# Two-layer decoder trunk, one core: which pairs of output tiles are multiplied by Strassen's scheme at the turns between stages

## Chip, cores, metric

One Trainium2 chip, one NeuronCore. The metric is device microseconds per execution; three executions of the kernel before took 2191.34, 2192.50 and 2198.03 us (median 2192.5).

## What is computed

Each of two layers does, for 512 prompt columns and 8 sample columns together (T = 520, D = 2048, fp32):

```
h = rmsnorm(x) * norm_g
z = h @ w_in
y_conv = B * conv3(C * xc) * silu(g_conv)
y_ret  = groupnorm(retention(q, k, v)) * silu(g_ret)
x = x + concat(y_conv, y_ret) @ w_out
x = x + sigmoid(x @ w_pg) * (p @ w_ple)
```

The four big products (w_in for the heads, w_in for the convolution, w_out, w_pg) hold nearly all the arithmetic.

## The kernel before, in words

Everything is held transposed: a tile is 128 features by 520 columns, and a matrix product has 16 input tiles (K tiles, KT = 16) and is made two output tiles at a time, a **pair**. Precision: every fp32 operand is split into a high and a low part (`split`, line 547; ACT writes the high part, DVE the rest), every weight tile too (`split_w`, line 226), and each product is three matmuls (`mm3`, lines 245 to 247) of 128x128 by 128x260, once for the LEFT and once for the RIGHT half of the columns.

A pair is made in one of two ways (`pair`, line 405). **Plain** (`plain`, line 281): K outermost, in four chunks of four K tiles; four PSUM banks are open from the first to the last chunk, and the banks are emptied only by whoever uses the result. It takes 16 x 4 x 3 = 192 matmuls. **Strassen** (`strassen`, line 303) with s of the 16 K tiles: seven products over s/2 K pairs, the rest of the K tiles plain, 192 - 1.5 s matmuls. It needs sums of weight tiles (DVE, line 328), sums of operand tiles (`operand_sums`, line 420: four DVE instructions of 128x260 per K pair; then `split_sums`, line 429: two ACT and two DVE instructions of 128x520), and inside the pair it moves banks about: `copy` and `plus` (traced at line 316) empty or duplicate banks on ACT and DVE, six ACT copies and two DVE additions where s is under 16, and the next product into that bank waits for them.

How many K tiles of each pair go by Strassen stands in tables: HEADS, CONVS, OUT_ROWS, GATES, one number per pair and layer, in the order in which the pairs run. The program runs heads, convolution, output projection (out), gate, and then the same for layer 1.

The operands of a stage are an `Operands` object with a list of things still to build (`todo`, lines 461 to 464): for each of 8 K pairs the split tiles, the sums, or both at once. `FIRST` says for how many tiles (4, so 2 K pairs) the sums are made together with the split tiles; the sums of the others come later from tiles that are loaded again, and have to be there before the first pair that uses them (`need`, line 494). `fill` builds ahead while enough of the 75 slots are free (it wants 7 above a reserve for a pair with sums). In the last pair of a stage the next stage's operands are built while its own are given back: `free` (line 517) gives back at steps 1, 3, 6, 7 and 8 of a Strassen pair, and all at the end of a plain one. `release` (line 504) gives back sums that no later pair uses. The final order on each engine is set by a scheduler from the program order, data and priorities; every engine then works through its own list in order.

The code of the pair and of what is built when:

```
first = max(rows[0], min(FIRST, max(rows))) // 2
self.todo = [(True, True)] * first + [(True, False)] * (KT // 2 - first)
...
self.todo += [(i, False, True) for i in range(first, max(rows) // 2)]
```

Of the kernel before, what the change touches and what calls it, by code (L numbers as in the profile page):

```python
# [47 lines left out]
SPREAD = (0, 6)  # L48


HEADS = [[0, 0, 0, 4, 8, 12] + [14] * 10, [4, 8, 12] + [14] * 13]
CONVS = [[14] * 2 + [16] * 13 + [14]] * 2
OUT_ROWS = [[0, 8, 16, 16, 16, 16, 16, 10]] * 2

MIXED, MIX = 64, [*range(8, 14), *range(8), 14, 15]
OUTS = [[MIXED + s for s in r] for r in OUT_ROWS]
GATES = [[4, 8, 12, 16, 16, 16, 16, 10], [4, 8, 12] + [14] * 4 + [0]]
WPRIO = 20
LATE = 0
RAW = 32  # L60
WARM = 8
FIRST = 4
SPLIT = 60


# [12 lines left out]
class Slots:  # L78
# [8 lines left out]
    def get(self, dtype=F32):  # L87
        i = self.free.pop(0)
        self.count += 1
        t = self.pool.tile([P, T], dtype, tag=f"s{i}", name=f"slot{i}_{self.count}")  # L90
        self.used[id(t)] = (t, i)
        return t
# [4 lines left out]
    def put(self, *slots):  # L97
        for t in slots:
            self.free.append(self.used.pop(id(t))[1])
# [90 lines left out]
def trunk_kernel(  # L190
# [17 lines left out]
    get, getr, put = slots.get, slots.getr, slots.put  # L208
# [22 lines left out]
    def chunks(a, b, most=CH):  # L231

        n = (b - a + most - 1) // most
        e = [a + (b - a) * i // n for i in range(n + 1)] if n else [a]
        return list(zip(e, e[1:]))

    def parts(src, a, b, slot=False):
        raw = load(src[:, P * a : P * b])
        w = split_w(raw, slot)
        raw_ring.put(raw)  # L240
        return w
# [9 lines left out]
    def product(out, w, c, xs, start, stop, more=False):  # L251

        for i, (xh, xl) in enumerate(xs):
            m = slice(P * (c + i), P * (c + i) + P)
            mm3(out, w[0][:, m], w[1][:, m], xh, xl, start and i == 0, stop and i == len(xs) - 1, more)

    def at(ops, ks, n):
        return [ops[k].view(n) for k in ks]

    def acc(n):  # L260
        return [banks.get() for _ in range(n)]

    def aside():

        if later:
            later.pop(0)()
# [11 lines left out]
            split_ring.put(*w)  # L278
        return Val(banks.put, ps=ps)

    def plain(x, src0, src1):

        ps = acc(4)
        for a, b in chunks(0, KT):
            x.supply(min(b + CH, KT))
            for i, src in enumerate((src0, src1)):
                w = parts(src, a, b)
                for j in range(a, b):
                    for h, n in enumerate((LEFT, RIGHT)):
                        product(ps[2 * i + h], w, j - a, at(x.ops, [j], n), j == 0, j == KT - 1)  # L290
                split_ring.put(*w)
            if b == KT // 2:
                while middle:
                    middle.pop(0)()
                aside()
        aside()
        return Val(banks.put, ps=ps[:2]), Val(banks.put, ps=ps[2:])
# [107 lines left out]
    def pair(x, src, m, n, nxt=None):  # L405


        s = x.rows[n]
        last = n == len(x.rows) - 1 and nxt is not None
        if s:  # L410
            z = strassen(x, src[m], src[m + 1], s, (lambda i: x.free(i, nxt)) if last else None)
        else:
            z = plain(x, src[m], src[m + 1])
            if last:
                x.free(8, nxt)
        x.release(n + 1)
        if nxt is not None and not last and not x.todo:
            nxt.fill(1, PRE)
        return z
# [14 lines left out]
    class Operands:  # L434


        def __init__(self, rows, load, reserve=0, whole=False, gain=None):
# [4 lines left out]
            self.ready = 0  # L442
            first = max(rows[0], min(FIRST, max(rows))) // 2
            self.todo = [(True, True)] * first + [(True, False)] * (KT // 2 - first)
# [72 lines left out]
        def free(self, i, nxt):  # L517

            s = self.rows[-1]
            if not self.whole:  # L520
                for n in range(s // 2):
                    x, y, t = self.ops[2 * n], self.ops[2 * n + 1], self.sums[n][4]
                    if i == 1 and x.halves:
                        put(*x.slots)
                        x.slots = []
                    if i == 3:
                        put(*t[:2])
                        del t[:2]
                    if i == 6:
                        put(*y.slots)  # L530
                        y.slots = []
                    if i == 7:
                        put(*t)
                        t.clear()
            if i == 8:
                self.drop()
            nxt.fill()

        def drop(self):
# [25 lines left out]
    def norm_g(l, k):  # L565
        return vec[:, 16 * l + k : 16 * l + k + 1]
# [97 lines left out]
    def from_dram(src):  # L664
        def load(k):
            t = get()
            SIDE.dma_start(t, src[k])
            return t

        return load  # L670

    xs = []
    X = Operands(HEADS[0][2:] + CONVS[0], from_dram(xT), gain=lambda k: norm_g(0, k))
    X.todo = [t for t in ((i, False, True) for i in range(max(X.rows) // 2))]
    X.ready = KT // 2
    rms = Rms()
    for a, b in ((0, 1), (1, 4), (4, 8), (8, 12), (12, 16)):
        raws = []
        if b == 1:
# [3 lines left out]
            x = get()  # L683
# [5 lines left out]
        else:  # L689
            for i in range(max(b - a, 3)):  # L690
                if i < 3:
                    raws.append(load(wi[0, i, :, P * a : P * b]))
                if i < b - a:
                    x = get()
# [24 lines left out]
    for l in range(DEPTH):  # L719
# [83 lines left out]
        def head(m):  # L803
            middle.append(lambda: X.fill(MORE_HEAD, 0))
            if m // 2 % 2:
                middle.append(sample)
            zs = pair(X, wi[l], m, m // 2 - skipped)
            X.fill(MORE_HEAD, 0)
            X.need(m // 2 - skipped + 1)
            sample()  # L810
            return zs
# [262 lines left out]

        O = Operands(OUT_ROWS[l], mixer, RESERVE_OUT)

        for j in range(CJ):
# [13 lines left out]
            t = get()  # L1091
# [37 lines left out]

        Gt = Operands(GATES[l][: (KT - tail) // 2], gate_in, RESERVE_GATE, whole=bool(tail))  # L1130
        for m in range(0, KT, 2):
# [20 lines left out]
        for k in range(2):  # L1152
            t = get()
# [20 lines left out]
        if not tail:  # L1174
            X = Operands(HEADS[l + 1] + CONVS[l + 1], next_in, RESERVE_NEXT, gain=lambda k, l=l: norm_g(l + 1, k))
        for m in range(0, KT - tail, 2):
# [10 lines left out]
            for i, z in enumerate(zs):  # L1187
                x = xs[i]
                t = get() if z.slot is None else z.slot
# [17 lines left out]
        if tail:  # L1207
# [53 lines left out]
            def update(x, pe, ps):  # L1261
                sg = get()
                t = sg[:, : x.shape[-1]]
                S.activation(t, ps, AF.Sigmoid)
                banks.put(ps)
                V.tensor_tensor(t, t, pe, MUL)
                V.tensor_tensor(x, x, t, ADD)
                return sg, t
# [5 lines left out]
            for i in range(tail):  # L1274
                ps = banks.get(TF)
                for c, w in enumerate(ws):
                    for k in range(2):
                        o, m = ops[2 * c + k], slice(PC * k + P * i, PC * k + P * i + P)
                        mm3(ps, w[0][:, m], w[1][:, m], o.x[:, n0], o.y[:, n0], c + k == 0, c + k == 8)
                x = x2[m0 + i][:, n0]  # L1280
                with tc.high_priority():
                    sg, t = update(x, pes[i][:, n0], ps)
# [15 lines left out]
            for j, n in enumerate(blocks):  # L1298
# [17 lines left out]
                x = xts[:, c]  # L1316
                with tc.high_priority():
                    sg, t = update(x, pts[:, c], ps)
# [147 lines left out]
```

## Time and profile before

| | |
|---|---|
| median of three executions | 2192.5 us |
| the profiled execution | 2188.46 us |
| its span on the core | 2186.6 us |
| mean granted TensorE clock | 0.997 of 2.4 GHz |
| matmuls recorded | 17870 |
| DMA, mean over the span | 179 GB/s |

The profiled execution lies 4.0 us under the median. Stages of the span: heads of layer 0 to about 460 us, convolution to 700, out from about 700 to 875, gate to 1090; heads of layer 1 to 1500, convolution to 1750, out to 1955, gate to the end. A *turn* below is the last pair of one stage and the first of the next.

### The profile page before, as it was taken

To read this page: it belongs to the slowest core of one execution; us is meant where nothing else is said; L and a number is where in the kernel's file an instruction comes from. 1 tells how busy PE (TensorE), PEld (TensorE's weight loads), DVE (VectorE), ACT (ScalarE), POOL (GpSimd) and SP (SyncE) were. 2 spreads that over 40 slices of the span, in tenths; PEclk is the share of its full clock that TensorE was granted. 3 is DMA by queue.
4 is the path that set the end of the run, shared out by engine and by line. 5 is a ranking of instruction groups with operands and counts; after the bars stand their busy time and mean duration, and the time that the engine had idled before them with its cause. 6 is when DMAs were issued, how large, how long until landed. Compare 5 with 4: busy or idle time off the path is not lost.

```text
span 2186.6 us, 48458 instructions
## 1 busy us (share of the span) xinstructions
PE 2155.9 (99%) x17870; PEld 2148.5 (98%) x17870; DVE 1902.8 (87%) x3910; ACT 1282.4 (59%) x2735; POOL 441.8 (20%) x764
## 2 busy tenths in 40 slices
PE   9999999999999999999999999999999999999998
PEld 8999999999999999999999999999999999999998
DVE  8789999899999988888897998989998999888874
ACT  8555666555555655655775565555645565455655
POOL 3213232211001311210211222222110032021011
PEclk9999999999999999999999999999999999999999
DMA  7656575545443853754645566664465456456455
GB/s 258 193 169 200 176 219 185 179 155 175 153 133 125 275 171 122 244 167 160 227 128 179 166 209 195 199 207 158 148 183 150 125 182 220 153 190 209 134 156 195
DMA packets 187918, 392.09 MB, mean 179 GB/s; under 512 B 26592, under 2 KB 66528, under 8 KB 187680
## 3 DMA queue, kind: packets, MB, share of 16 engines
q1 hardware_dynamic: 133040, 214.30, 31.4%
q0 software_dynamic: 54496, 174.62, 24.0%
q8 instruction: 140, 2.29, 0.4%
q14 instruction: 98, 0.80, 0.1%
q10 hardware_dynamic: 144, 0.08, 0.0%
HBM read 323.74 MB, written 65.15 MB: 178 GB/s over the span
## 4 chain that ended last, share of the span: by engine, by line
PE 86%; DMA 5%; issue 3%; ACT 3%; DVE 3%; POOL 1%; SPq 0%; DVEq 0%; ACTq 0%; POOLq 0%
PE ps_g L245 27%; PE ps_g L247 27%; PE ps_g L246 27%; DMA raw<-wg 1%; ACT split L227 1%; DVE split L228 1%; DMA o_rets<-slot 1%; DMA slot<-x2s 1%; DMA slot<-xT 1%; ACT slot L553 1%; DMA raw<-wi 0%; DVE raw L328 0%; POOL slot L1060 0%; DMA raw<-wo 0%; ACT slot L476 0%
## 5 line engine op out<-in xcount | busy, mean ns | idle before, releaser
L245 PE MATMUL ps_g<-slot,split 128*128 128x260 f32 x5500 | 1543.0, 284 | 18.5 <-ACT ps_g L316 8.1
L246 PE MATMUL ps_g<-slot,split 128*128 128x260 f32 x5500 | 1546.1, 283 | 0.3 <-DVE slot L557 0.3
L247 PE MATMUL ps_g<-slot,split 128*128 128x260 f32 x5496 | 1531.4, 283 | 0.6 <-DVE split L228 0.6
L227 ACT ACTIVATE split<-raw 128x512 fp32r<-128x512 f32 (+2 forms) x1388 | 783.2, 584 | 618.5 <-DVE raw L328 199.8
L245 PEld LDWEIGHTS ps_g<-slot,split 128*128 128x128 f32 x5500 | 1031.5, 189 | 22.9 <-ACT ps_g L316 9.2
L246 PEld LDWEIGHTS ps_g<-slot,split 128*128 128x128 f32 x5500 | 1036.7, 189 | 0.5 <-DVE slot L557 0.5
L247 PEld LDWEIGHTS ps_g<-slot,split 128*128 128x128 f32 x5496 | 1028.0, 189 | 0.9 <-DVE split L228 0.8
L228 DVE TENSOR_TENSOR split<-raw,split 128x512 fp32r<-128x512 f32 (+2 forms) x1387 | 848.5, 633 | 182.6 <-ACT split L227 112.8
L328 DVE TENSOR_TENSOR raw<-raw 128x512 f32<-128x512 f32 (+2 forms) x680 | 427.1, 640 | 20.3 <-DMA raw<-wi 13.5
L316 ACT ACTIVATE slot<-ps_g 128x260 f32<-128x260 f32 x360 | 135.6, 379 | 125.2 <-PE ps_g L247 110.5
L554 DVE TENSOR_TENSOR slot<-slot,slot 128x520 fp32r<-128x520 f32 (+1 forms) x206 | 120.3, 615 | 3.9 <-ACT slot L553 3.1
L553 ACT ACTIVATE slot<-slot 128x520 fp32r<-128x520 f32 (+1 forms) x206 | 106.6, 565 | 12.5 <-DVE slot L425 4.4
L783 POOL DMA_DIRECT2D o_rets<-slot x64 | 35.4, 553 | 338.5 <-DVE slot L782 121.3
L316 DVE TENSOR_TENSOR slot<-ps_g,slot 128x260 f32<-128x260 f32 x180 | 75.9, 422 | 5.9 <-PE ps_g L247 3.8
L1060 POOL DMA_DIRECT2D slot<-x1s x82 | 44.0, 538 | 144.1 <-DVE slot L554 51.7
L871 POOL DMA_DIRECT2D slot<-hs x64 | 46.2, 723 | 112.5 <-PE ps_st L247 31.0
L316 ACT ACTIVATE ps_g<-ps_g 128x260 f32<-128x260 f32 x140 | 52.1, 372 | 19.1 <-PE ps_g L247 18.6
L741 DVE TENSOR_TENSOR slot<-slot,slot 128x520 f32<-128x520 f32 x80 | 55.5, 693 | 8.8 <-DMA o_rets<-slot 7.8
L782 DVE SCALAR_TENSOR_TENSOR slot<-slot,vs,slot 128x256 f32<-128x256 f32 x128 | 56.0, 478 | 7.0 <-ACT slot L778 6.3
L816 POOL DMA_DIRECT2D hs<-slot x64 | 35.6, 557 | 129.9 <-DVE slot L757 59.7
L772 POOL DMA_DIRECT2D slot<-sret x64 | 35.3, 552 | 131.4 <-ACT split L227 33.4
L773 POOL DMA_DIRECT2D slot<-kq x64 | 34.8, 544 | 118.6 <-DVE slot L1109 18.2
(217 smaller groups left out, 1667.4 us busy)
## 6 DMA issues: line engine op xcount, KB each, us to landing
raw<-wi SPq DMA_DIRECT2D x377, 256.0 KB, 3.9
raw<-wo SPq DMA_DIRECT2D x112, 256.0 KB, 4.9
raw<-wi SPq DMA_DIRECT2D x136, 192.0 KB, 3.9
raw<-wg SPq DMA_DIRECT2D x88, 256.0 KB, 4.9
slot<-x1s POOLq DMA_DIRECT2D x82, 260.0 KB, 5.8
slot<-sret POOLq DMA_DIRECT2D x64, 256.0 KB, 4.0
hs<-slot POOLq DMA_DIRECT2D x64, 256.0 KB, 3.9
slot<-hs POOLq DMA_DIRECT2D x64, 256.0 KB, 5.1
```

The lines of the kernel that those rows point to most:

```text
L227: S.activation(hi, raw, AF.Copy)
L228: V.tensor_tensor(lo, raw, F(hi), SUB)
L245: PE.matmul(out, wh, xh, start=start, stop=False, skip_group_check=more)
L246: PE.matmul(out, wh, xl, start=False, stop=False, skip_group_check=more)
L247: PE.matmul(out, wl, xh, start=False, stop=stop, skip_group_check=more)
L316: fn(*args)
L328: V.tensor_tensor(out[:, n], x[:, n], y[:, n], op)
L553: keep(S.activation(hi, src[:, n], AF.Copy))
L554: V.tensor_tensor(lo, src[:, n], F(hi), SUB)
L741: V.tensor_tensor(out[:, n], v, table[:, n], MUL)
L782: keep(V.scalar_tensor_tensor(st[:, c], k, vs[:, h, e, b : b + 1], st[:, c], MUL, ADD))
L871: SIDE.dma_start(t[:, :512].rearrange("p (m n) -> p m n", m=2), src)
```

## The change

The tables get other numbers: the last out pair and the last gate pair of layer 0 become plain (10 to 0), the first gate pair of both layers and the first head pair of layer 1 become plain (4 to 0), and the pairs that come after these go to their full number at once (16, 14) instead of by 8 and 12. In layer 0's heads 4, 8, 12 becomes 8, 14, 14. FIRST goes from 4 to 8: the sums of the first four K pairs are made together with their split tiles. A last plain pair now gives back its operands chunk by chunk (`free_tiles`).

```
-HEADS = [[0, 0, 0, 4, 8, 12] + [14] * 10, [4, 8, 12] + [14] * 13]
+HEADS = [[0, 0, 0, 8] + [14] * 12, [0] + [14] * 15]
 CONVS = [[14] * 2 + [16] * 13 + [14]] * 2
-OUT_ROWS = [[0, 8, 16, 16, 16, 16, 16, 10]] * 2
+OUT_ROWS = [[0, 8, 16, 16, 16, 16, 16, 0]] * 2
...
-GATES = [[4, 8, 12, 16, 16, 16, 16, 10], [4, 8, 12] + [14] * 4 + [0]]
+GATES = [[0, 16, 16, 16, 16, 16, 16, 0], [0, 16, 16] + [16] * 4 + [0]]
...
-FIRST = 4
+FIRST = 8
...
-    def plain(x, src0, src1):
+    def plain(x, src0, src1, step=None):
...
                 split_ring.put(*w)
+            if step:
+                step(a, b)
...
-            z = plain(x, src[m], src[m + 1])
-            if last:
-                x.free(8, nxt)
+            z = plain(x, src[m], src[m + 1], (lambda a, b: x.free_tiles(a, b, nxt)) if last else None)
...
+        def free_tiles(self, a, b, nxt):
+            for t in self.sums:
+                put(*t[4])
+                t[4] = []
+            for op in self.ops[a:b]:
+                put(*op.slots)
+                op.slots = []
+            nxt.fill()
```

Line numbers behind line 281 move by 2 to 9 in the changed kernel (L316 becomes L318, L553 becomes L562, L554 L563, L1140 L1149, L1191 L1200).

ACT at the turn from layer 0's gate to layer 1's heads, before: L476 scales an operand tile of the heads, L553 writes the high part of one, L227 splits weights, L1191 is the sigmoid of the last gate pair, and `ps_g<-ps_g` is the copy that duplicates a bank inside the first head pair.

```order
L476 ACTIVATE slot_794_14109<-slot_794_14109,vec 128x520
L553 ACTIVATE slot_795_14132<-slot_793_14107 128x260
L553 ACTIVATE slot_796_14133<-slot_793_14107 128x260
L227 ACTIVATE split<-raw 128x256
L553 ACTIVATE slot_771_13958<-slot_769_13952 128x260
L553 ACTIVATE slot_772_13959<-slot_769_13952 128x260
L553 ACTIVATE slot_773_13964<-slot_770_13954 128x520
L227 ACTIVATE split<-raw 128x512
L476 ACTIVATE slot_810_14292<-slot_810_14292,vec 128x520
L1191 ACTIVATE slot_758_13856<-slot_758_13856 128x520
L316 ACTIVATE ps_g<-ps_g 128x260
```

The same engine at the same turn in the changed kernel; L1200 reads the banks of the last gate pair directly.

```order
L562 ACTIVATE slot_801_14100<-slot_798_14008 128x520
L562 ACTIVATE slot_771_13886<-slot_764_13867 128x520
L562 ACTIVATE slot_781_13912<-slot_775_13896 128x520
L562 ACTIVATE slot_789_13986<-slot_786_13922 128x520
L227 ACTIVATE split<-raw 128x512
L562 ACTIVATE slot_783_13916<-slot_776_13897 128x520
L1200 ACTIVATE slot_803_14158<-ps_g 128x260 x2
L227 ACTIVATE split<-raw 128x512
L476 ACTIVATE slot_816_14224<-slot_816_14224,vec 128x520
L476 ACTIVATE slot_815_14222<-slot_815_14222,vec 128x520
L476 ACTIVATE slot_791_13990<-slot_791_13990,vec 128x520
L1200 ACTIVATE slot_805_14169<-ps_g 128x260 x2
```

No bank copy stands at this turn any more; the first one of the stage comes after both plain pairs, and the high parts of operand sums (slots 771, 781, 783) stand before the sigmoids.

DVE at the turn from layer 0's out to its gate, before: L228 splits weights, L1140 adds the residual to an out tile, L426 and L427 are operand sums, L554 writes the low part of an operand or of a sum.

```order
L1140 TENSOR_TENSOR slot_585_11109<-slot_587_11116,slot_585_11109 128x520
L228 TENSOR_TENSOR split<-raw,split 128x256
L426 TENSOR_TENSOR slot_605_11398<-slot_599_11360,slot_598_11358 128x260
L427 TENSOR_TENSOR slot_605_11398<-slot_599_11360,slot_604_11397 128x260
L554 TENSOR_TENSOR slot_606_11403<-slot_598_11358,slot_606_11403 128x260
L554 TENSOR_TENSOR slot_608_11407<-slot_599_11360,slot_607_11406 128x520
L228 TENSOR_TENSOR split<-raw,split 128x384
L1140 TENSOR_TENSOR slot_586_11110<-slot_588_11117,slot_586_11110 128x520
L554 TENSOR_TENSOR slot_591_11343<-slot_571_10405,slot_591_11343 128x260
L554 TENSOR_TENSOR slot_593_11347<-slot_572_10407,slot_592_11346 128x520
L554 TENSOR_TENSOR slot_595_11351<-slot_589_11337,slot_594_11350 128x520
```

DVE inside the last out pair of layer 0 in the changed kernel (the residual additions of the pair before it stand ahead of these rows, its own come some 40 rows later).

```order
L563 TENSOR_TENSOR slot_587_11325<-slot_583_11315,slot_587_11325 128x260
L563 TENSOR_TENSOR slot_588_11326<-slot_583_11315,slot_588_11326 128x260
L563 TENSOR_TENSOR slot_590_11332<-slot_584_11317,slot_589_11331 128x520
L425 TENSOR_TENSOR slot_599_11413<-slot_596_11345,slot_599_11413 128x260
L426 TENSOR_TENSOR slot_600_11414<-slot_596_11345,slot_595_11343 128x260
L563 TENSOR_TENSOR slot_592_11336<-slot_585_11319,slot_591_11335 128x520
L563 TENSOR_TENSOR slot_594_11340<-slot_586_11320,slot_593_11339 128x520
L427 TENSOR_TENSOR slot_600_11414<-slot_596_11345,slot_599_11413 128x260
L228 TENSOR_TENSOR split<-raw,split 128x512
L563 TENSOR_TENSOR slot_604_11426<-slot_596_11345,slot_603_11425 128x520
L424 TENSOR_TENSOR slot_611_11441<-slot_609_11437 128x260
L426 TENSOR_TENSOR slot_612_11442<-slot_610_11439,slot_609_11437 128x260
```

Gate operands and gate sums now stand between the weight splits of the last out pair itself, and the additions of weight tiles (L328 before) are gone from it.

## Rows read from the trace of the kernel before

**Rows 1.** The page's first part: busy us, share of the span, instructions.

```profile
PE 2155.9 (99%) x17870; PEld 2148.5 (98%) x17870; DVE 1902.8 (87%) x3910; ACT 1282.4 (59%) x2735; POOL 441.8 (20%) x764
```

**Rows 2.** Busy us and records by stretch: PE, PEld, DVE, ACT, POOL, PEclk, DMA, GB/s.

```profile
50.00:100.00 50.00, 50.00 (x413) 49.50 (x413) 38.36 (x78) 25.01 (x54) 14.34 (x27) 1.00 0.60 191
100.00:150.00 50.00, 50.00 (x420) 50.00 (x419) 41.95 (x88) 30.30 (x66) 7.31 (x14) 1.00 0.46 142
740.00:760.00 20.00, 19.39 (x162) 19.18 (x161) 17.84 (x39) 9.64 (x21) 3.78 (x7) 1.00 0.61 186
860.00:930.00 70.00, 65.49 (x527) 64.66 (x526) 58.25 (x130) 42.14 (x95) 17.67 (x33) 0.98 0.64 215
1080.00:1116.00 36.00, 30.74 (x238) 29.85 (x238) 33.17 (x78) 33.71 (x71) 10.82 (x18) 0.95 0.67 232
1795.00:1840.00 45.00, 43.50 (x357) 42.79 (x356) 40.54 (x88) 26.60 (x66) 12.57 (x24) 1.00 0.76 267
1950.00:2010.00 60.00, 56.55 (x468) 55.93 (x467) 51.62 (x105) 38.43 (x80) 17.65 (x33) 1.00 0.69 242
```

**Rows 3.** Waits of PE over the span: us in total, times, longest.

```profile
PE ps_g L245 <- ACT ps_g L316: 8.1, 4, 4.2
PE ps_g L245 <- ACT slot L316: 7.5, 7, 1.3
```

**Rows 4.** Timeline of ACT, then of PE, at the turn to layer 1's heads.

```profile
1090.30 0.72 ACT L476 ACTIVATE slot<-slot,vec 128x520 f32<-128x520 f32 x1
1090.91 0.72 ACT L553 ACTIVATE slot<-slot 128x260 fp32r<-128x260 f32 x2
1091.53 0.41 ACT L227 ACTIVATE split<-raw 128x256 fp32r<-128x256 f32 x1
...
1092.98 0.62 ACT L227 ACTIVATE split<-raw 128x512 fp32r<-128x512 f32 x1
1093.51 0.72 ACT L476 ACTIVATE slot<-slot,vec 128x520 f32<-128x520 f32 x1
1094.12 0.63 ACT L1191 ACTIVATE slot<-slot 128x520 f32<-128x520 f32 x1
1094.65 0.38 ACT L316 ACTIVATE ps_g<-ps_g 128x260 f32<-128x260 f32 x1
1094.95 0.63 ACT L553 ACTIVATE slot<-slot 128x520 fp32r<-128x520 f32 x1
...
1095.08 0.58 PE L245 MATMUL ps_g<-slot,split 128*128 128x260 f32 x1 [4.16 <-ACT ps_g L316]
```

**Rows 5.** Two stretches of 5 us after that wait, columns as in rows 2.

```profile
1095.00:1100.00 5.00, 4.92 (x29) 4.92 (x30) 5.00 (x14) 5.00 (x12) 0.54 (x1) 0.68 0.46 158
1100.00:1105.00 5.00, 5.00 (x44) 5.00 (x43) 5.00 (x12) 5.00 (x10) 1.08 (x2) 1.00 0.43 104
```

**Rows 6.** Timeline of DVE at the turn from out to gate, layer 0.

```profile
871.80 0.55 DVE L228 TENSOR_TENSOR split<-raw,split 128x384 fp32r<-128x384 f32 x1
872.27 0.69 DVE L1140 TENSOR_TENSOR slot<-slot,slot 128x520 f32<-128x520 f32 x1
872.88 0.42 DVE L228 TENSOR_TENSOR split<-raw,split 128x256 fp32r<-128x256 f32 x1
873.22 0.42 DVE L426 TENSOR_TENSOR slot<-slot,slot 128x260 f32<-128x260 f32 x1
873.56 0.42 DVE L427 TENSOR_TENSOR slot<-slot,slot 128x260 f32<-128x260 f32 x1
...
899.10 1.28 DVE L228 TENSOR_TENSOR split<-raw,split 128x512 fp32r<-128x512 f32 x2
900.30 0.42 DVE L424 TENSOR_TENSOR slot<-slot 128x260 f32<-128x260 f32 x1
```

## The prediction

> **What bounds the kernel now.** I read the busy shares first [rows 1]: TensorE (PE) is busy 99% of the span, DVE 87%, ACT 59%. The reader is to take from this only that TensorE sets the time; pipelined matmuls hide small delays in a busy share. So the second view counts matmuls by stretch. In an undisturbed stretch 420 start in 50 us (100 to 150) [rows 2], 8.4 per us or 0.119 us each. Against that rate the other stretches are short by a number that can be turned into time:
>
> - from out to gate, layer 0 (860 to 930): 70 x 8.4 = 588, there are 527, 61 short, 7.3 us;
> - from gate to layer 1's heads (1080 to 1116): 302 against 238, 64 short, 7.7 us. Some 0.7 us of it is my estimate for the norm's own slow matmuls: layer 0's norm spread falls in 50 to 100, which has 413 records where 420 would be, 0.8 us. So 7.0 us can be had;
> - from out to gate, layer 1 (1950 to 2010): 504 against 468, 36 short, 4.3 us;
> - from convolution to out: 6 short in 740 to 760, 0.7 us, and 21 short in 1795 to 1840, 2.5 us [rows 2].
>
> The third view says on what TensorE waits: in 11 cases, 15.6 us in all, on the bank copies of Strassen's scheme on ACT (L316) [rows 3]. The fourth shows why [rows 4]: the copy at 1094.65 is a 0.3 us instruction, but ACT works in order, and ahead of it stand operand tiles of the heads, weight splits and a sigmoid; TensorE waited 4.16 us for it. After that wait the granted clock is 0.68 over 5 us, that is, part at 1.2 GHz: 29 records where the next 5 us hold 44, 15 x 0.119 = 1.8 us more [rows 5].
>
> **The change, part by part.** The sum is made against the profiled execution (2188.5 us, span 2186.6), which lies 4.0 us under the median of the runs.
>
> *Matmuls.* A pair takes 192 - 1.5 s. Summing s over the tables: layer 0 heads 164 to 176, layer 1 heads 206 to 210, out 98 to 88 in each layer, gate 98 to 96 and 80 to 96; 744 to 754 in all. Ten more give 15 matmuls less: 15 x 0.119 = **-1.8 us**.
>
> *The three turns.* Advance per instruction, from start to start. ACT: 0.61 us for a scaled 128x520 tile, 0.31 for 128x260 or 128x256, 0.53 for 128x512 or an unscaled 128x520, 0.30 for a bank copy [rows 4]; 0.42 for 128x384, halfway. DVE: 0.61 for 128x520, 0.34 for 128x256 and 128x260, 0.47 for 128x384, 0.60 for 128x512 [rows 6].
>
> From gate to heads, over the last gate pair and the first head pair. Before, TensorE has 177 + 186 = 363 matmuls, 43.2 us. ACT: weight splits 12.2 (seven products of 2 and 3 tiles, 7 x 0.73, four splits of 3 tiles; seven of 2 tiles, six of 4), bank copies 12 x 0.30 = 3.6, scaling 16 x 0.61 = 9.8, high parts 8 x 1.15 = 9.2, the four sums that the second head pair wants 8 x 0.53 = 4.2, tiles scaled again for two of them 2.4, sigmoids and squares 2.1: 43.5 us. DVE: weights 13.6, weight sums 4.6, bank additions 1.4, low parts 8 x 1.29 = 10.3, four sums at 4 x 0.34 + 2 x 0.61 = 2.58, 10.3, gate and norm 3.9: 44.1 us. Both engines have more to do than TensorE, 101% and 102%.
>
> After, 384 matmuls, 45.7 us. ACT: weights 16 x 0.53 = 8.5, no copies, 9.8 and 9.2 as before, seven sums now wanted before the second pair 7.4, tiles scaled again for three 3.7, sigmoids, squares and the head's copies 3.5: 42.1 us, 92%. DVE: weights 9.6, low parts 10.3, seven sums 18.1, gate and norm 3.9: 41.9 us, 92%. So the sums that move forward eat most of what weight sums and copies give back, but both engines come under TensorE, and no matmul of these two pairs waits for a bank copy. What is late next: the four banks of the last gate pair, plus one that the embedding's product holds, are all five, and the second half's sigmoids stand behind one weight split and three scaled tiles, 0.53 + 3 x 0.61 + 2 x 0.31 = 3.0 us, against 24 matmuls (2.9 us) that need only the first half's banks. I leave 2.5 us of 7.0 (between 0 and all of it; nearer to 0, since 3.8 us of both engines are free now): **-4.5 us**.
>
> From out to gate, DVE before: 13.6 + 4.6 + 1.4 + 10.3 + 10.3 + 1.2 (residual) + 1.2 (embedding operands) = 42.6 of 43.2 us, 99%. After: weights 9.6, low parts 10.3, all eight sums 20.6, residual 1.4, embedding 1.2: 43.1 of 45.7 us, 94%; ACT has 27 us. I leave 1.5 us in each layer, of 7.3 and 4.3 (from 0 to all): **-5.8** and **-2.8 us**. The clock falls inside these stretches go with the waits.
>
> *From convolution to out.* The out pairs 0 and 8 stay, but FIRST puts two more sums, 2 x 2.58 = 5.2 us of DVE, ahead of the later tiles. In the new order the second out pair's first product stands 78 matmuls after the first pair's, where it stood 219 after, so TensorE is given that pair's work while tiles 8 to 15 are made. Bounds: the 0.7 and 2.5 us of now gone, or 5.2 us more at each. I take **0**, nearer to the first end, because DVE's work over these pairs is the same before and after, only in another order.
>
> *Layer 0's heads.* Four sums are wanted where two were, then seven where four were: at most 3 x 2.58 = 7.7 us of DVE earlier. DVE is busy 38.4 and 42.0 of 50 us there [rows 2], 19.7 us free in 100: **0**, and 7.7 us if that cover were not free. *DMA.* Sums made with their operands spare a second load of tiles, and the plain pairs issue fewer weight loads; queues are 0.64 to 0.69 filled at the turns [rows 2]: **0**. *The end* (gate of layer 1 to the last store) keeps its code: **0**.
>
> Sum: -1.8 - 4.5 - 5.8 - 2.8 = -14.9 us; 2173.6 for an execution like the profiled one, 2177.6 for the median.
>
> **A rule against the count.** In the three stretches PEld (weight loads) is idle 5.3, 6.2 and 4.1 us, 15.6 us [rows 2], where the count gives 18.6. The difference is half-clock time: 1095 to 1100 shows PEld 4.92 of 5 us busy with 15 records missing [rows 5]. The Trainium skill (Perfetto Trace Analysis, Identifying the Most-Contended Engine) calls the share of time in LDWEIGHTS a good measure of how far TensorE is from its limit. By that rule the three terms would be 15.6 - 5.5 = 10.1 us and the median 2180.6; the trace speaks against it for as long as the clock is down.
>
> **Rivals.**
>
> *Moved, not removed in part.* The second pair of each stage wants seven or eight sums where it wanted four, and DVE is at 92 to 94%. If half of the 18.6 us comes back as a wait of the second pair's products on sums: -1.8 - 9.3, 2181.4 us. For it: the loads. Against: ACT's copies, on which 15.6 us of waits were written [rows 3], are gone from both pairs.
>
> *Nothing but the count.* All stall time comes back, at second pairs and at banks: 2190.7 us. This is also what comes out if the scheduler does not let the builds run ahead; the DVE rows of the last out pair speak against that, since gate sums stand between its weight splits.
>
> *Slower.* The builds wait for slots. A pair with sums wants 7 free slots above a reserve of 8 or 10 and keeps 8. If the free ones are used up until the second half of the last plain pair has given its tiles back, DVE has 45.7 - 11.4 = 34.3 us for 41.9 to 43.1 us of work: 7.6, 8.8 and 8.8 us late, 25.2, and a clock fall of 1.8 at each, 30.6 us. Less the 20.4 that go: +10.2, 2202.7 us. It decides from about 9 us of lateness per turn. Against: `release` gives back all 32 slots of sums before that pair starts, where it was 12.
>
> **How the numbers follow.** About 0.3% (6.6 us) is what a measurement of this kernel can tell from no change. Forecast 0.70, half moved 0.13 (both faster), nothing but the count 0.11 (same), slots 0.06 (slower). Faster 0.83, same 0.11, slower 0.06. The range: down to where the 18.6 us, the 3.2 us from convolution to out and the 1.8 all go, 2168.9; up over the half-moved case to 2188, which leaves out the slots and most of the case of the count.
>
> **What would show it.** Right: the waits of TensorE on L318 copies drop from 15.6 us to under 6; in the three turns 8.2 or more matmuls per us; no stretch with granted clock under 0.9 between 50 us and the end; about 15 matmul records less. Wrong: a wait of several us in the second gate or head pair on a low part of a sum (DVE L563) or on its copy; DVE idle at a turn with the pool queue waiting for a slot; a first out pair that waits on operand tiles 8 to 15.

## The result, and the profile after

Four executions of the changed kernel took 2178.23 to 2182.75 us, median 2178.4; the kernel before, on the same chip, had a median of 2193.9. The ratio is 0.9932 with a 95% interval of 0.9912 to 0.9953: faster, by 0.5 to 0.9%. In a later comparison (e0) the ratio was 0.9949 (0.9936 to 0.9962). The forecast was 2177.6, so the total came out as predicted; that it did so to 1 us is partly luck (see "The sum" below). Its terms did not all: the turns gave more than was forecast, and two places that were put at nothing took 3.4 us each.

The profiled execution took 2178.3 us, with a span of 2176.5, 10.1 us less than the span of before. (The medians differ by 15.5; the profiled execution of before lies 5.5 us under the median of the four runs of before in this comparison.)

The first part of the page, and the waits of TensorE over the span (us in total, times, longest), answering to [rows 1] and [rows 3]:

```profile
PE 2152.1 (99%) x17855; PEld 2145.0 (99%) x17855; DVE 1898.7 (87%) x3849; ACT 1264.4 (58%) x2656; POOL 435.4 (20%) x746
```

```profile
PE ps_g L245 <- ACT split L227: 4.7, 5, 2.0
PE ps_g L245 <- ACT slot L318: 4.4, 5, 1.9
PE ps_g L245 <- ACT slot L565: 1.5, 2, 1.0
PE ps_g L245 <- ACT ps_g L318: 1.4, 3, 0.8
```

There are 15 matmuls less, as counted. The waits on bank copies (L318) went from 15.6 us to 4.4 + 1.4 = 5.8. At the head now stand 4.7 us on weight splits (ACT L227); the longest of these, 2.0 us, stands from convolution to out, at 734.59.

The stretches of [rows 2], in the changed kernel (same columns: PE, PEld, DVE, ACT, POOL, PEclk, DMA, GB/s), and then four where it got worse:

```profile
860.00:930.00 70.00, 70.00 (x586) 70.00 (x586) 61.54 (x126) 43.64 (x86) 18.28 (x34) 1.00 0.69 224
1080.00:1116.00 36.00, 35.92 (x301) 35.72 (x299) 34.26 (x80) 30.91 (x64) 10.56 (x15) 1.00 0.49 151
1950.00:2010.00 60.00, 60.00 (x503) 60.00 (x502) 54.06 (x106) 36.71 (x67) 12.54 (x24) 1.00 0.65 212
...
50.00:100.00 50.00, 48.12 (x383) 47.43 (x383) 40.30 (x80) 26.54 (x55) 14.74 (x27) 0.97 0.61 185
...
90.00:95.00 5.00, 3.46 (x29) 3.25 (x28) 0.00 (x0) 0.50 (x2) 0.00 (x0) 1.00 0.99 355
95.00:100.00 5.00, 4.65 (x26) 4.65 (x27) 4.88 (x9) 1.45 (x4) 0.00 (x0) 0.66 0.11 40
...
730.00:735.00 5.00, 2.41 (x18) 2.03 (x17) 5.00 (x12) 5.00 (x20) 1.07 (x2) 1.00 1.03 392
```

At 8.4 per us the first three would hold 588, 302 and 504: the 61, 64 and 36 matmuls that were missing are 2, 1 and 1. In 50 to 100, where 413 started before, 383 start now, and 730 to 735 holds 18 where 42 would be.

For the experiments the same reading is made by pairs, so that it does not hang on where a stretch is cut: **lost time** is the time from the start of one pair's first matmul to that of a later pair's, less 0.119 us for each matmul between. It contains waits, slow clock, and the norm's own 0.7 us. The columns begin and end at the same pairs in every kernel; in the kernel before that is, for layer 0's heads, 81 to 151 us, convolution to out about 703 to 850 and 1782 to 1930, out to gate 870 to 972 and 1951 to 2050, gate to heads 1088 to 1183 (it begins with the first head pair). By the same count of matmuls the stages change at about 383, 724, 897 and 1088 us in layer 0 and at 1462, 1803 and 1974 in layer 1, not where the list of stages ahead of the prediction puts them. The entries are good to some 0.3 us. Records are those of the trace, all else is in us:

| kernel | records | heads, layer 0 | conv. to out, 0 | out to gate, 0 | gate to heads | conv. to out, 1 | out to gate, 1 | the rest | lost, all |
|---|---|---|---|---|---|---|---|---|---|
| before | 17870 | 0.7 | 2.0 | 7.8 | 9.2 | 3.4 | 5.0 | 28.9 | 57.1 |
| changed | 17855 | 4.1 | 5.4 | 0.6 | 3.7 | 3.2 | 0.7 | 30.3 | 48.1 |
| e0 changed, again | 17855 | 4.1 | 5.7 | 0.6 | 2.7 | 3.2 | 0.7 | 30.5 | 47.5 |
| e1 last pairs only | 17915 | 0.7 | 2.2 | 2.1 | 2.9 | 3.7 | 2.1 | 28.7 | 42.3 |
| e2 first pairs only | 17828 | 0.7 | 2.5 | 3.7 | 8.6 | 3.6 | 4.8 | 35.7 | 59.6 |
| e5 freed at the end | 17855 | 4.1 | 5.5 | 0.7 | 2.1 | 3.4 | 0.7 | 31.1 | 47.4 |
| e6 low parts twice | 17855 | 4.2 | 15.9 | 6.2 | 9.7 | 15.9 | 2.7 | 30.3 | 84.8 |
| e8 high parts twice | 17855 | 4.6 | 10.2 | 0.7 | 9.4 | 9.0 | 0.7 | 28.9 | 63.6 |
| e4 old heads, layer 0 | 17873 | 0.7 | 2.6 | 0.6 | 2.9 | 1.7 | 0.7 | 31.2 | 40.3 |
| e9 larger raw ring | 17855 | 0.9 | 5.5 | 0.7 | 2.1 | 5.4 | 0.6 | 34.5 | 49.6 |
| e3 FIRST 4 | 17855 | 2.9 | 3.9 | 0.8 | 4.3 | 1.8 | 0.7 | 28.5 | 42.8 |
| e7 old heads, FIRST 4 | 17873 | 0.7 | 2.8 | 0.8 | 4.5 | 2.9 | 0.8 | 29.6 | 42.0 |

The three turns lost 22.0 us before and 5.0 now: 17.0 gained. Layer 0's heads and convolution to out lose 3.4 us more each, the rest 1.4, convolution to out in layer 1 0.2 less. Net -9.0, and -1.8 for the matmuls; against the 10.1 us of the span, 0.7 us more stand behind the last matmul.

### The profile page after: what moved, and what is told of

It is laid out like the page before. It is cut to its first block, busy times and chain, and to the rows that moved or that the text cites. A ratio compares the mean times of both kernels' runs of the same rounds, so it can differ in the third digit from the quotient of the medians.

```text
span 2176.5 us, 48167 instructions
## 1 busy us (share of the span) xinstructions
PE 2152.1 (99%) x17855; PEld 2145.0 (99%) x17855; DVE 1898.7 (87%) x3849; ACT 1264.4 (58%) x2656; POOL 435.4 (20%) x746
## 5 line engine op out<-in xcount | busy, mean ns | idle before, releaser
L227 ACT ACTIVATE split<-raw 128x512 fp32r<-128x512 f32 (+2 forms) x1346 | 779.0, 597 | 601.4 <-DVE raw L330 204.3
L228 DVE TENSOR_TENSOR split<-raw,split 128x512 fp32r<-128x512 f32 (+2 forms) x1345 | 845.6, 648 | 178.4 <-PE ps_g L246 87.7
L330 DVE TENSOR_TENSOR raw<-raw 128x512 f32<-128x512 f32 (+1 forms) x660 | 427.3, 657 | 31.3 <-DMA raw<-wi 23.4
L318 ACT ACTIVATE slot<-ps_g 128x260 f32<-128x260 f32 x336 | 127.4, 381 | 138.0 <-PE ps_g L247 121.8
L562 ACT ACTIVATE slot<-slot 128x520 fp32r<-128x520 f32 (+1 forms) x212 | 109.4, 563 | 41.6 <-DVE slot L425 9.1
L563 DVE TENSOR_TENSOR slot<-slot,slot 128x520 fp32r<-128x520 f32 (+1 forms) x212 | 122.6, 607 | 1.7 <-ACT slot L562 1.7
L318 DVE TENSOR_TENSOR slot<-ps_g,slot 128x260 f32<-128x260 f32 x168 | 70.5, 421 | 5.9 <-PE ps_g L247 3.2
L825 POOL DMA_DIRECT2D hs<-slot x64 | 35.7, 558 | 143.1 <-DVE slot L766 72.8
L1210 POOL DMA_DIRECT2D x2s<-slot x30 | 16.4, 547 | 208.6 <-DVE slot L1205 207.6
```

The lines of the kernel that those rows point to most:

```text
L227: S.activation(hi, raw, AF.Copy)
L228: V.tensor_tensor(lo, raw, F(hi), SUB)
L318: fn(*args)
L330: V.tensor_tensor(out[:, n], x[:, n], y[:, n], op)
L562: keep(S.activation(hi, src[:, n], AF.Copy))
L563: V.tensor_tensor(lo, src[:, n], F(hi), SUB)
```

## Experiments

**e0: the changed kernel again.** No edit.

> The changed kernel once more, so that the other kernels stand beside it on the same chip: 0.993 of before, and the same waits in its trace as in the first profile, near 95 us (1.9 us, layer 0's heads), 711, 731 and 735 us (3.4 us together, convolution to out), 2139 and 2144 us. If those come from the order in the program, they return at the same instructions; if they come from one execution's transfers, other ones stand there.

2178.0 us against 2189.2 for before on this chip, 0.9949 (0.9936 to 0.9962), a little less gain than the 0.993 that was expected. The waits stand at the same instructions: near 96 us (1.9 us), 713, 732 and 736 (1.3, 0.6, 2.0), 2139 and 2143. So they belong to the program's order. Gate to heads, 3.7 and 2.7, shows how far one execution may stray: differences of over 1 us in the table can be read.

**e1 and e2: which of the two plain pairs of a turn does it.**

e1, against the changed kernel (last pairs plain, all else as before):

```
-HEADS = [[0, 0, 0, 8] + [14] * 12, [0] + [14] * 15]
+HEADS = [[0, 0, 0, 4, 8, 12] + [14] * 10, [4, 8, 12] + [14] * 13]
-GATES = [[0, 16, 16, 16, 16, 16, 16, 0], [0, 16, 16] + [16] * 4 + [0]]
+GATES = [[4, 8, 12, 16, 16, 16, 16, 0], [4, 8, 12] + [14] * 4 + [0]]
-FIRST = 8
+FIRST = 4
```

> Only the last pairs of out and of layer 0's gate are plain, with their tiles given back by fours; first pairs, FIRST and both layers' heads as before. 45 matmuls more than before: +5.4 us (17915 records). Theory 1 (each stall belongs to the bank copies of the very pair in which it stands): the waits of the last pairs near 876, 890, 1090 and 1956 go, 7.9 us with the slow clock behind the first; the wait of 4.2 us near 1095, at the first head pair's copies, stays with its 1.6 us of slow clock, as do those of the second gate pairs (1.4 us each). -2.5 us against before, about 2191 us median. Theory 2 (the two engines had 101 and 102% of TensorE's time over the two pairs, and the stall is that excess): with one pair plain ACT has 39 and DVE 37 of 45 us from gate to heads, so the wait near 1095 goes as well, to under 1 us: 16 us less waiting, 5.4 more matmuls, about 2183 us.

e2 (first pairs plain, FIRST 8, last pairs and layer 0's heads as before):

```
-HEADS = [[0, 0, 0, 8] + [14] * 12, [0] + [14] * 15]
+HEADS = [[0, 0, 0, 4, 8, 12] + [14] * 10, [0] + [14] * 15]
-OUT_ROWS = [[0, 8, 16, 16, 16, 16, 16, 0]] * 2
+OUT_ROWS = [[0, 8, 16, 16, 16, 16, 16, 10]] * 2
-GATES = [[0, 16, 16, 16, 16, 16, 16, 0], [0, 16, 16] + [16] * 4 + [0]]
+GATES = [[0, 16, 16, 16, 16, 16, 16, 10], [0, 16, 16] + [16] * 4 + [0]]
```

> Only the first pairs of both gates and of layer 1's heads are plain, with FIRST 8; the last pairs keep s = 10 and layer 0's heads are as before. 42 matmuls fewer than before: -5.0 us (17828 records). Theory 1 (each stall belongs to the copies of its own pair): the wait near 1095 (4.2 us and 1.6 us of slow clock) and the one near 1977 (1.2) go, those near 876 (2.2), 890, 1090 and 1956 stay; from convolution to out 3.3 us are lost as in the changed kernel; -8.7 us, about 2185 us. Theory 2 (excess of ACT and DVE over the two pairs): from gate to heads ACT has 45.7 and DVE 48.7 us of work against 43.9 of matmuls, since seven sums are wanted and the weight sums and copies of s = 10 stay, so 4.8 us or more are still lost there, and as much or more from out to gate (DVE 49.7 against 43.9); -1.7 us or worse, 2192 us or above.

e1 took 2178.2 us beside 2189.7 for before, 0.9944 (0.9931 to 0.9956); e2 2186.2, 0.9988 (0.9980 to 0.9997). e1 follows theory 2: it lies 11.5 us under before, where theory 2 had 10.6 (16 less waiting, 5.4 more matmuls) and theory 1 had 2.5. e2's total doesn't decide: 3.4 us under before, between theory 1 (8.7) and theory 2 (1.7, or worse). What decides there is the loss from gate to heads: theory 1 took 5.8 of the 9.2 us away, theory 2 left 4.8 or more, and 8.6 are lost. (From out to gate in layer 0 it loses 3.7, less than theory 2 had.) The stretch 1080 to 1116 in e1, then 1100 to 1150 in e2, and TensorE's waits in e1:

```profile
1080.00:1116.00 36.00, 35.37 (x290) 34.69 (x289) 33.38 (x75) 29.95 (x63) 9.44 (x16) 1.00 0.60 194
```

```profile
1100.00:1150.00 50.00, 47.47 (x368) 45.83 (x367) 45.60 (x93) 28.76 (x65) 13.63 (x19) 0.97 0.40 119
```

```profile
PE ps_g L245 <- ACT slot L318: 3.4, 6, 1.1
...
PE ps_g L245 <- ACT ps_g L318: 2.0, 4, 0.6
```

(The second view is e2's, 1100 to 1150: there its loss stands, 368 records where 420 would be.) In e1 the first head pair still goes by s = 4, with the same bank copy that TensorE waited 4.16 us for [rows 4]; the longest wait on such a copy is now 0.6 us. So that copy was late because of the work that the gate pair ahead of it had left on ACT and DVE, not because it was there. e2 takes the copy away and keeps the s = 10 pair ahead: 8.6 us stay lost where 9.2 were. It loses 7.5 us more than before further on, between 1177 and 1464 us, at two places in the same way. ACT at the first:

```profile
1230.05 0.42 ACT L227 ACTIVATE split<-raw 128x256 fp32r<-128x256 f32 x1 [3.79 <-DMA raw<-wi]
1230.37 0.37 ACT L318 ACTIVATE ps_g<-ps_g 128x260 f32<-128x260 f32 x1
```

A split that waits 3.79 us for its weights stands ahead of a bank copy, and TensorE waits 2.2 us for the copy; again near 1283. This is the shape of the stall in layer 0's heads (e4 and e9).

What then do the plain first pairs bring? e4 (below) is e1 plus these pairs and FIRST 8. It has 42 records less, 5.0 us, and its median is 5.2 us lower (2173.0 and 2178.2, same comparison). Together with FIRST 8, then, their gain is the matmuls; the waits of the second gate pairs that they remove (1.1 us each in e1, at 923 and 1997) are offset elsewhere.

**e5: are the slots given back by fours what matters?**

```
-            z = plain(x, src[m], src[m + 1], (lambda a, b: x.free_tiles(a, b, nxt)) if last else None)
+            z = plain(x, src[m], src[m + 1])
+            if last:
+                x.free(8, nxt)
```

> The changed kernel, but a last plain pair gives its operand slots back all at once behind its last product and not by fours. Theory of the load (the turns were lost because ACT and DVE had more work than TensorE over two pairs): the work is the same, so the turns stay nearly clean, at most 2 us more lost in all, within 0.1% of the changed kernel. Theory of the slots (what a plain last pair brings is room to build the next operands while it still runs): the next stage's sums can't be made until the pair ends, DVE has 34 of 46 us for 42 us of work, 7.6 to 8.8 us late at each of the three turns, with DVE idle in the last pair and the pool queue waiting for slots: 15 to 25 us more, 2190 us or above.

2176.1 us, 0.9937 (0.9925 to 0.9950), beside 2178.0 for the changed kernel: no loss at all, and the turns as clean. The slots do not set the turns, so the prediction's slower rival had no ground; `free_tiles` itself brings nothing that these runs show.

**e6 and e8: a known dose on DVE alone, and on ACT alone.** In `split`, for operand tiles only:

```
                 keep(S.activation(hi, src[:, n], AF.Copy))
+                if twice:
+                    keep(S.activation(hi, src[:, n], AF.Copy))
                 V.tensor_tensor(lo, src[:, n], F(hi), SUB)
+                if twice:
+                    V.tensor_tensor(lo, src[:, n], F(hi), SUB)
```

(e8 has the first two added lines, e6 the last two.)

> The changed kernel with the low part of every operand tile of out, gate and layer 1's heads written twice by DVE: the same values, 16 x 0.65 = 10.3 us more of DVE at each turn, nothing on ACT or TensorE. Theory of the load: DVE then has 53.4 us from out to gate and 52.2 from gate to heads, TensorE 45.7, so 6.5 to 7.7 us are lost again at each of the three turns (0.4, 2.6 and 0.4 in the changed kernel), and about as much where convolution goes to out: 20 to 30 us more, 2195 to 2205 us. Rival (the work of DVE is not what sets the turns; the bank copies on ACT were, and they are gone from those pairs): most of it hides, under 2 us more at each turn, under 2183 us.

> The changed kernel with the high part of every operand tile of out, gate and layer 1's heads written twice by ACT: the same values, 16 x 0.55 to 0.61 = 8.8 to 9.8 us more of ACT at each turn, nothing on DVE. Theory of the load, by the prediction's sums: from gate to heads ACT then has 51 to 52 of TensorE's 45.7 us, so 5 to 6 us are lost again there; from out to gate it has 37 of 45.7, so nothing is lost there in either layer (under 1 us); from convolution to out, where ACT is busy some 14 to 15 of 20 us, 0 to 5 us in each layer. Together +5 to +16 us against the changed kernel, 2183 to 2194 us. Rival (only DVE's work sets the turns): under 1.5 us more at gate to heads too.

e6 took 2212.9 us, 1.011 (1.0096 to 1.0124); e8 2193.3, 1.0018 (1.0009 to 1.0027). e8 lies in the range expected; e6 costs 35 us over e0, more than the 20 to 30 expected, and the excess stands from convolution to out. Gate to heads and convolution to out in e6, then the three turns in e8, with the slow clock at gate to heads on lines of its own:

```profile
1080.00:1116.00 36.00, 33.31 (x270) 32.80 (x269) 36.00 (x81) 31.27 (x63) 10.27 (x20) 0.96 0.73 230
1115.00:1120.00 5.00, 4.92 (x22) 4.92 (x23) 5.00 (x13) 3.26 (x7) 0.91 (x2) 0.50 0.50 168
...
715.00:760.00 45.00, 35.85 (x260) 34.55 (x260) 44.30 (x98) 24.47 (x70) 10.67 (x20) 0.89 0.66 215
```

```profile
860.00:930.00 70.00, 70.00 (x586) 69.92 (x585) 58.66 (x118) 49.81 (x105) 17.14 (x32) 1.00 0.69 220
1080.00:1116.00 36.00, 31.46 (x241) 30.41 (x240) 29.57 (x64) 34.88 (x76) 9.79 (x19) 0.91 0.58 181
1100.00:1105.00 5.00, 1.16 (x4) 0.93 (x5) 4.48 (x11) 5.00 (x11) 0.54 (x1) 0.69 0.53 150
1105.00:1110.00 5.00, 4.92 (x26) 4.33 (x26) 4.10 (x10) 5.00 (x11) 0.00 (x0) 0.63 0.00 0
1950.00:2010.00 60.00, 60.00 (x503) 60.00 (x502) 51.69 (x101) 43.40 (x81) 14.98 (x28) 1.00 0.74 234
```

Against e0, gate to heads loses 7.0 us more with 10.3 us of DVE added and 6.7 more with some 9 of ACT, so neither dose is free there. Up to 3.4 us of each loss is slow clock (1110 to 1125 in e6, 1100 to 1110 in e8). TensorE's waits in 1080 to 1150 come to 4.0 us in e6 and 4.5 in e8, to 0.4 in e0: some 6 to 7 us of the DVE dose and 5 of the ACT dose fit in, more than the 3.8 that the prediction worked out. From out to gate the ACT dose is free in both layers (586 and 503 records, as without it), and the DVE dose costs 5.6 us in layer 0 and 2.0 in layer 1. So the engines come out as in the prediction's sum, 94% for DVE and 27 of 45.7 us for ACT, but DVE has more room than it said, in layer 1 above all. The dose also shows the tightest place, which the prediction had not weighed: from convolution to out it costs 10.2 and 12.7 us on DVE, up to 5.1 of either by slow clock, and 4.5 and 5.8 on ACT. In 715 to 760 DVE was busy 42 of 45 us before and after (kernel before, then the changed one):

```profile
715.00:760.00 45.00, 44.39 (x370) 44.18 (x369) 42.30 (x90) 27.72 (x75) 14.19 (x27) 1.00 0.81 284
...
715.00:760.00 45.00, 42.41 (x351) 41.98 (x351) 42.28 (x91) 27.54 (x78) 12.33 (x23) 1.00 0.74 248
```

**e4 and e9: the stall in layer 0's heads.** In the changed kernel ACT, and then SP (the queue that issues the weight loads), near 95 us:

```profile
87.15 0.71 ACT L787 ACTIVATE slot<-slot,vec 128x512 f32<-128x512 f32 x1
94.50 0.52 ACT L227 ACTIVATE split<-raw 128x384 fp32r<-128x384 f32 x1 [6.64 <-DMA raw<-wi]
94.93 0.37 ACT L318 ACTIVATE slot<-ps_g 128x260 f32<-128x260 f32 x1
```

```profile
60.00 4.05 SPq L220 DMA_DIRECT2D raw<-wi  x2
83.11 7.49 SPq L323 DMA_DIRECT2D raw<-wi  x8
```

```profile
SPq L323 <- DVE raw L330: 18.9, 1, 18.9
```

SP waits 18.9 us for the ring of raw weight tiles, then issues the eight loads of the first s = 14 pair within 7.5 us, 1.8 MB. They take a median of 7.6 us to land, with the queues 0.99 full and 355 GB/s moved in 90 to 95. (Part of that traffic is POOL's own loads and stores, in e9 as well.) ACT, in order, stands 6.64 us in front of the first of those splits, and behind it stands the bank copy of the pair that is running. TensorE waits 1.88 us for that copy, and then the clock is at half speed in part of the next 5 us (26 records, granted 0.66).

e4, against the changed kernel:

```
-HEADS = [[0, 0, 0, 8] + [14] * 12, [0] + [14] * 15]
+HEADS = [[0, 0, 0, 4, 8, 12] + [14] * 10, [0] + [14] * 15]
```

> The changed kernel with layer 0's heads as before (0, 0, 0, 4, 8, 12, then 14). 18 matmuls more: +2.1 us (17873 records). If the stall of the changed kernel at 95 us (1.9 us of waiting, then granted clock 0.66) comes from the step from s = 8 straight to 14, where eight loads of seven weight tiles are issued at once (SP held 18.9 us by the ring of raw weights) and land 10 us late: the stall goes, no stretch of 5 us between 60 and 300 has a clock under 0.9, lost time in pairs 3 to 6 falls by 3.4 us; net -1.3 us, about 2177 us, and 100 us after the start of the program as before's. If it comes from another part of the change (nothing else differs ahead of 300 us), it stays: 2180.5 us.

e9:

```
-RAW = 32
+RAW = 40
-SPLIT = 60
+SPLIT = 56
```

> The changed kernel with a ring of 40 raw weight tiles in place of 32 and, to pay for it, 56 split tiles in place of 60. If the stall at 95 us comes from the ring (the seven-tile loads for the first s = 14 pair have no place until the s = 8 pair's tiles are summed at 83 us, and ACT's queue holds the s = 8 pair's bank copy behind the first of their splits): the loads of the first seven-tile product issue before 83 us, ACT waits less than 2 us for raw weights between 85 and 96, TensorE's wait of 1.9 us near 95 and the clock of 0.66 behind it go, 3 us less lost in pairs 3 to 6; about 2175 us. If it comes from the order on ACT or from the sums, whatever the ring holds, the wait near 95 stays at 1 us or more.

e4: 2173.0 us, 0.9920 (0.9907 to 0.9934), no stall, 0.7 us lost in these pairs. It lies 4 us under the 2177 expected, since convolution to out loses less too (see e3). e9 keeps the tables and changes only the rings, and the stall goes too (0.9 us lost). SP, ACT and a stretch of 5 us in e9:

```profile
64.02 23.98 SPq L323 DMA_DIRECT2D raw<-wi  x8
```

```profile
89.56 0.53 ACT L227 ACTIVATE split<-raw 128x384 fp32r<-128x384 f32 x1 [1.24 <-PE ps_g L246]
90.04 0.39 ACT L318 ACTIVATE slot<-ps_g 128x260 f32<-128x260 f32 x1
```

```profile
95.00:100.00 5.00, 5.00 (x44) 5.00 (x43) 5.00 (x14) 1.06 (x3) 1.09 (x2) 1.00 0.17 59
```

The same eight loads are spread over 24 us, and the same copy runs at 90.04 and not at 94.93. So the raw ring is the cause (the split ring that pays for it only gets smaller), and what decides is when the loads can be issued. As a whole e9 gains nothing: 2181.7 us where 2175 was expected, 0.9965 (0.9952 to 0.9977). It loses 2.2 us more from convolution to out in layer 1, and 4 more in the rest; whether that is the smaller ring of split tiles or another order is not shown.

**e3 and e7: FIRST.** One line each, FIRST 8 to 4; e7 has e4's heads as well.

> The changed kernel with FIRST 4 in place of 8. If the 3.3 us that layer 0 loses more from convolution to out (710 to 740) come from the two further sums that FIRST 8 puts ahead of the later operand tiles: they go, and the stretch 700 to 750 is near before's again (no waits of over 0.5 us near 711, 731, 735). At the turns the sums of pairs 4 to 8 are made from second loads, scaled again on ACT: 2.4 us more of ACT from gate to heads, 44.5 of 45.7 us: 0 to 2 us more lost there. Together -3 to +1 us against the changed kernel, 2175 to 2179 us. Rival (the loss near 711 to 735 is the plain pair's weight loads and tiles meeting, whatever FIRST is): the waits there stay at 3 us or more, 2178 to 2181 us.

> The changed kernel with layer 0's heads as before and FIRST 4: only the plain pairs of the turns are left of the change. If both edits act where the earlier runs showed it (no stall at 95 us with the old heads, less lost from convolution to out with FIRST 4), they don't add up in full, since the old heads alone already left only 1.7 us lost from convolution to out: 2170 to 2173 us beside 2189.7 for before, 0.991 to 0.9925. Rival (FIRST 8 spares second loads and scaling at the turns): 1 to 3 us slower than with the old heads alone, 2174 to 2176 us.

e3: 2171.8 us, 0.9919 (0.9905 to 0.9932), under both ranges. Its layer 0 heads lose 2.9 us where the changed kernel loses 4.1, with the same stall: TensorE waits 2.2 us near 96, but the clock stays up behind it.

```profile
PE ps_g L245 <- ACT slot L318: 2.2, 1, 2.2
...
95.00:100.00 5.00, 4.31 (x36) 4.32 (x37) 4.54 (x9) 1.79 (x4) 0.00 (x0) 1.00 0.23 85
```

So 1.2 us of e3's gain is the clock and not an effect of FIRST that its trace shows. Convolution to out in layer 0 loses 3.9 instead of 5.4 to 5.7 us: the waits near 731 and 735 go, that of 0.8 us near 711 stays. In e4, with FIRST 8 and the old heads, the one near 711 is gone and little is left of the others (2.6 us lost). So neither theory holds as it was put: the full 3.4 us need both the new heads and FIRST 8, and the new heads with FIRST 4 keep 1.9 of them. That the two edits act through the order of DVE's and ACT's lists is argued, not shown: in 730 to 735 both engines are busy all the 5.00 us, and the longest wait is for a weight split on ACT. Which instruction there decides stays open. e7: 2173.4 us, 0.9924 (0.9912 to 0.9936), between its two forecasts, 4.6 us under e0 in the same comparison, and not better than e3 or e4 alone: they do not add up. What FIRST 8 spares at gate to heads may show, 2.9 us lost in e4 and 4.5 in e7, but 3.7 and 2.7 came from one and the same kernel.

e3, e4 and e7 lie within 2 us of each other. e7 was timed beside the changed kernel, and its runs (2169.4 to 2174.3) lie under all of e0's (2175.2 to 2181.1): it beats both kernels.

## Why the prediction was right, and where it was not

- **Matmuls, -1.8.** Right: 15 records less.
- **The three turns, -4.5, -5.8 and -2.8.** Lost time fell by 5.5, 7.2 and 4.3, 17.0 where 13.1 was forecast. The mechanism was right: e1, e6 and e8 show that the work of ACT and DVE over the two pairs sets these turns, at gate to heads on both engines, from out to gate on DVE. The terms mis-sized are the remainders: 2.5 us from gate to heads and 1.5 us at each turn from out to gate were left standing, and in the three forecast stretches 1, 2 and 1 matmuls are missing, 0.1 to 0.2 us each. One reason was put wrongly: "no matmul of these two pairs waits for a bank copy" counts the first pair's copies among what had to go, and e1 keeps them without the wait. It is the plain last pair that pays, and the first one pays by its count.
- **Layer 0's heads, 0.** The step that failed. It asked only whether DVE could make three sums earlier, and DVE could. It did not ask what the raw ring does when a pair of four-tile products is followed by one of seven: +3.4 us (e9 shows the ring as cause).
- **DMA, 0.** Failed in the same place. The share over 50 to 100 us is 0.60 before [rows 2] and 0.61 after, and says nothing of a burst of 0.99 over 5 us in it.
- **Convolution to out, 0, bounds to +5.2 in each layer.** +3.4 in layer 0, inside the bounds, and -0.2 in layer 1. The reason for taking 0 ("DVE's work over these pairs is the same before and after, only in another order") was wrong where it stood: DVE is busy 42 of 45 us, and ACT all of 730 to 735, where TensorE waits longest; an order that fits less well costs time there. Which part of the order it is stays open (e3).
- **The end and all else, 0.** +1.4 us, 0.8 of it behind layer 1's last gate pair, where TensorE now waits 1.2 us at 2139 and 1.7 at 2144 on ACT, and 0.7 more behind the last matmul (7.3 us before, 7.9 now). The code of the end is the same, as the prediction says, but the gate pairs ahead of it are not: GATES takes layer 1's from s = 14 to 16. Whether that moves the waits is not shown.
- **The sum.** -14.9 us was forecast; -10.1 came between the two profiled executions. The median was met because the profiled execution of before lies further under its median than the prediction took (5.5 us, not 4.0) and that of the changed kernel does not (0.1 us). Beside e0 the medians lie 11.2 us apart. So the change is worth about 10 to 11 us by these two counts, and that the median came out so near the forecast is luck in part: a gain larger than forecast at the turns and losses that were not forecast nearly cancel, and the execution that was profiled did the rest.
- **Rivals.** "Moved in part to the second pair" did not happen: the second gate pairs lose nothing any more, the second head pair of layer 1 only a wait of 0.4 us (near 1124), and what came back came in other stages. "Nothing but the count" is out with the 17.0 us. "Slots" is refuted by e5.
- **The rule against the count.** The Trainium skill (Perfetto Trace Analysis, Identifying the Most-Contended Engine) would read the gain of the three stretches off the idle time of weight loads: 15.6 us before, 0.3 now, 15.3. The count gives 161 matmuls less 4, 18.7 us, and the lost time by pairs 17.0. Where the clock falls the difference is plain: in e6, 715 to 760, weight loads are idle 10.5 us, and 118 of 378 matmuls are missing, 14.0 us, at a granted clock of 0.89. The count stays the better measure there.
- **What would show it.** Waits on copies under 6 us: 5.8. At least 8.2 per us at the turns: 8.4. No stretch under 0.9 of the clock: wrong, 95 to 100 has 0.66, and 2145 to 2150 at the end has 0.74.

## What to carry to other kernels

When TensorE waits for a short instruction on an in-order engine, add up what stands ahead of that instruction over the last two pairs, on both helper engines, and lighten the pair ahead; taking away the instruction that it waits for may do nothing (e2). Before making an early step larger, ask of each ring when its first load can be issued, not only whether the engines have time. A known dose on one engine alone (e6, e8) tells in one run how much room each turn has, if the slow clock that the dose brings is counted apart from the waits.

## What was not expected of the hardware

Two waits of the same length, in one trace, left different clocks. Behind the wait of 1.88 us at 95.35 the clock fell; behind that of 1.95 us at 734.59 it did not. The granted clock was 1.00 in the stretch of each wait, 90 to 95 and 730 to 735. Then, in steps of 2 us:

```profile
734.00:736.00 2.00, 1.41 (x11) 1.41 (x12) 2.00 (x6) 1.27 (x5) 0.90 (x2) 1.00 0.99 331
736.00:738.00 2.00, 2.00 (x19) 2.00 (x18) 2.00 (x6) 0.00 (x0) 0.00 (x0) 1.00 0.79 251
...
96.00:98.00 2.00, 2.00 (x12) 2.00 (x12) 1.97 (x5) 0.93 (x2) 0.00 (x0) 0.54 0.10 31
98.00:100.00 2.00, 2.00 (x13) 2.00 (x13) 2.00 (x5) 0.00 (x0) 0.00 (x0) 0.61 0.00 0
```

96 to 98 and 98 to 100 hold 12 and 13 records where 736 to 738 holds 19, and a granted 0.54 and 0.61 means that the engine ran at 1.2 GHz for most of these 4 us. e0 repeats both: 0.73 in 95 to 100 and 1.00 in 735 to 740, each with a wait of 1.9 to 2.0 us. In e3 the wait near 96 is longer, 2.2 us, and the clock stays at 1.00; in e2 it fell behind the wait of 2.19 us at 1230.8 (0.66 in 1230 to 1235) and stayed at 1.00 behind that of 2.16 us at 1282.8. The price of such a wait is therefore either its length, or its length and some 1.5 us more (3.4 us were lost in layer 0's heads, 1.9 of them waiting), and no row here tells beforehand which.
